# Column sums of the modulation rows: the rows as stationary operand against a column of ones, in place of a selector product, a copy and a transpose

## The chip, the core and the metric

The kernel runs on one core of one Trainium2 chip. The metric is the device time of one execution in microseconds (us), as a median of several runs. All arithmetic of the parts named here is in f32.

## What is computed

The program runs two layers of a diffusion backbone on 128 context tokens and 256 latent tokens. Before each sub-layer the normalised tokens are scaled and shifted by a modulation that depends on one vector per token group, `c_ctx` for the context and `c` for the latents. The part of the reference that matters here:

```
def modulate(h, shift, scale):
    return h * (1 + scale) + shift

def adaln(cvec, w, b):
    mod = jnp.einsum('nd,de->ne', jax.nn.silu(cvec), w) + b
    return jnp.split(mod[:, None, :], 6, axis=-1)

def trunk_layer(x, mods, mixer_w, g_norm_l, w_gu_l, w_down_l, ctx):
    sh1, sc1, ga1, sh2, sc2, ga2 = mods
    h = modulate(rms_norm(x, g_norm_l[0]), sh1, sc1)
    mix, new_ctx = token_mixers(h, *mixer_w, ctx)
    x = x + ga1 * rms_norm(mix, g_norm_l[1])
    f = swiglu(modulate(rms_norm(x, g_norm_l[2]), sh2, sc2), w_gu_l, w_down_l)
    x = x + ga2 * rms_norm(f, g_norm_l[3])
    return x, new_ctx
```

`w` is 1024 x 6144 in each layer. The six vectors sh1, sc1, ga1, sh2, sc2, ga2 are numbered 0 to 5 in the kernel (`vec`). Shifts and scales (0, 1, 3, 4) are wanted as columns, with the feature on the partition, since the tokens they act on lie transposed. The gates (2, 5) are wanted as rows.

## The kernel before

The class `Ada` computes the modulation piece by piece, in half vectors of 512 features. `issue` (L157 and on) loads four chunks of `w_ada`, 256 rows each. What follows depends on the stage.

In the token mixers `mul_p` multiplies on TensorE and sums over rows there; that path ends in `cols`, which the change splits in two without changing what it issues.

In the channel mixer (`ffn`) of both layers `mul_v` multiplies on ScalarE (the first row block) and VectorE (`scalar_tensor_tensor`, L179, seven for each of two token groups). The products pile up in `acc`, 128 partitions x 2 groups (`s`) x 512 features, which lies in one of two spare buffers (`spare` in the profile). Then the 128 partitions must be summed: `sum_v`. It takes eight f32 products, two groups `s` by four slices `g` of 128 features. The stationary operand is `pick`, 128 x 32, zero but for one column of ones; the moving operand is `acc`. Row `32 g + s` of the tile `adap` so receives the sum of slice g for group s. For a shift or scale VectorE then copies these rows to SBUF (L196), and one step later `cols` transposes them on TensorE (L233, tile `adat`) and adds the bias from the transposed tile into `Bmod` (L237) or `Amod` (L240, L242). For a gate VectorE adds a bias and `gate` goes on with the rows.

`ffn` of the first layer computes the gate 5 of its own layer and the vectors 0, 1, 3, 4 of the second layer, two halves each: ten calls of `sum_v`, two of them for gates. `ffn` of the second layer has the two gate halves alone. So the copy, the transpose and `cols` after a `sum_v` occur eight times in the program, all in the channel mixer of the first layer.

That stage also runs the channel mixer's own products. Each f32 value is split in a high and a low part (f32r), and each product takes three matmuls, `mm3` (L108 to L110): `gups` (gate and up, 128 x 384 tokens, weights from `ring` and `xring`) and `facc` (down, 128 x 512). ScalarE and VectorE split the weights into `hi` and `lo` or into the rings (L118, L119, L1209, L1210), and form `sg` and `f` between gate/up and down (L1223 to L1227).

What sets the order: `tick` issues one chunk, runs one deferred step from `later`, and then multiplies one chunk. In this stage a tick may do both. The stage is laid out by a scheduler; the instructions of each engine run in the order that it gives them, and each waits by semaphore for what it reads and for the buffer it writes. PSUM tiles `gups`, `adap` and `adat` share two buffers (tag `gu`), in turn.

Of the kernel before, what the change touches and what calls it, by code (L numbers as in the profile page):

```python
# [12 lines left out]
ALU = mybir.AluOpType  # L13
# [39 lines left out]
def hybrid_step(  # L53
# [8 lines left out]
    V, A, PE, G, SP = nc.vector, nc.scalar, nc.tensor, nc.gpsimd, nc.sync  # L62
# [17 lines left out]
    ident = cst[:, C_ID:C_ID + 128]  # L80
# [12 lines left out]
    gbn = cp.tile([128, 2, 2, 128], F32, name="gbn")  # L93
    G.memset(gbn, 0.0)
    pick = cp.tile([128, 33], F32, name="pick")
# [48 lines left out]
    class Ada:  # L144
# [38 lines left out]
            self.later += [lambda: self.sum_v(l, vec, half, acc)]  # L183

        def sum_v(self, l, vec, half, acc):
            ps = self.ps("adap")[:, 0:128]
            for s in range(2):
                for g in range(4):
                    PE.matmul(ps[32 * g:32 * g + 32], lhsT=pick[:, 1 - s:33 - s], rhs=acc[:, s, g * 128:(g + 1) * 128],
                              start=s == 0, stop=s == 1)  # L190
            rows = ap_.tile([128, 128], F32, tag="acc", name="acc", bufs=2)
            if vec in (2, 5):
                V.tensor_tensor(rows, ps, gbn[:, half, 0], ALU.add)
                self.gate(l, vec, half, rows)
            else:
                V.tensor_copy(rows, ps)  # L196
                self.later.insert(0, lambda: self.cols(l, vec, half, rows))

        def gate(self, l, vec, half, acc):

# [26 lines left out]
                    self.later += [lambda: self.cols(l, vec, half, acc)]  # L227

        def cols(self, l, vec, half, acc):
            which = 0 if vec < 3 else 1  # L230
            ks = slice(half * 4, half * 4 + 4)
            ps = self.ps("adat")
            PE.transpose(ps[:, 0:128], acc, ident)  # L233
            pv = ps[:, 0:128].rearrange("p (k r) -> p r k", k=4)[:, 0:2]
            bc = bcol[:, l, vec, ks].unsqueeze(1).broadcast_to([128, 2, 4])
            if vec in (0, 3):
                V.tensor_tensor(Bmod[:, l, which, :, ks], pv, bc, ALU.add)  # L237
            else:
                am = Amod[:, l, which, :, ks]
                V.tensor_tensor(am, pv, bc, ALU.add)  # L240
                gc = gcol[:, l, 2 * which, ks].unsqueeze(1).broadcast_to([128, 2, 4])
                V.scalar_tensor_tensor(am, am, 1.0, gc, ALU.add, ALU.mult)  # L242
# [1237 lines left out]
```

## Time and profile before

| what | us |
|---|---|
| median of 3 runs | 1000.54 |
| lowest and highest run | 1000.4, 1001.1 |
| the profiled execution's own time | 1001.41 |
| its span in the trace, first to last instruction | 999.6 |
| TensorE busy in the span | 966.1 |
| VectorE busy | 623.3 |
| ScalarE busy | 466.8 |

The profiled execution has 1.8 us outside its span. A busy TensorE is not TensorE at its peak: matmuls are pipelined, and the profile's rows overlap. What a piece costs on the path is therefore read from the chain of waits, whose rows do not overlap, and from the starts of consecutive matmuls, not from the length of a row. An f32 product appears as two weight loads (engine PEld) and two matmuls (engine PE); an f32r product and a transpose appear as one of each.

### The profile page before, as it was taken

To read this page: it belongs to the slowest core of one execution; us is meant where nothing else is said; L and a number is where in the kernel's file an instruction comes from. 1 tells how busy PE (TensorE), PEld (TensorE's weight loads), DVE (VectorE), ACT (ScalarE), POOL (GpSimd) and SP (SyncE) were. 2 spreads that over 40 slices of the span, in tenths; PEclk is the share of its full clock that TensorE was granted. 3 is DMA by queue.
4 is the path that set the end of the run, shared out by engine and by line. 5 is a ranking of instruction groups with operands and counts; after the bars stand their busy time and mean duration, and the time that the engine had idled before them with its cause. 6 is when DMAs were issued, how large, how long until landed. Compare 5 with 4: busy or idle time off the path is not lost.

```text
span 999.6 us, 16493 instructions
## 1 busy us (share of the span) xinstructions
PE 966.1 (97%) x6537; PEld 838.9 (84%) x6537; DVE 623.3 (62%) x1036; ACT 466.8 (47%) x930; POOL 85.8 (9%) x142
## 2 busy tenths in 40 slices
PE   5999999999999999999999999999999999999997
PEld 3789886668999999999987898766899999999996
DVE  3566657767964979986265757677787533333323
ACT  4545537678533433333266346577873323333322
POOL 0312320000000200000010343000000000000000
PEclk8999999999999999999999999999999999999999
DMA  9958678407873777763033794430575344333001
GB/s 327 314 175 255 207 211 237 150 1 253 277 231 126 265 256 236 252 229 110 22 100 107 189 283 122 110 106 1 191 270 192 127 149 148 127 127 127 22 1 64
DMA packets 128414, 167.30 MB, mean 167 GB/s; under 512 B 15600, under 2 KB 90080, under 8 KB 128336
## 3 DMA queue, kind: packets, MB, share of 16 engines
q1 hardware_dynamic: 122112, 154.00, 48.2%
q0 software_dynamic: 5856, 12.09, 4.4%
q8 instruction: 51, 0.84, 0.4%
q14 instruction: 27, 0.22, 0.1%
q10 hardware_dynamic: 368, 0.16, 0.1%
HBM read 163.51 MB, written 2.70 MB: 166 GB/s over the span
## 4 chain that ended last, share of the span: by engine, by line
PE 84%; ACT 5%; DVE 4%; DMA 3%; issue 2%; SPq 1%; POOL 0%; ACTq 0%; DVEq 0%; POOLq 0%
PE gups L108 11%; PE gups L110 11%; PE gups L109 11%; PE facc L108 6%; PE facc L110 6%; PE facc L109 6%; PE tps L108 3%; PE fps L108 2%; PE tps L110 2%; PE tps L109 2%; PE fps L110 2%; PE fps L109 2%; PE ops L108 2%; PE adap L214 2%; PE ptp L1031 2%
## 5 line engine op out<-in xcount | busy, mean ns | idle before, releaser
L119 DVE TENSOR_TENSOR lo<-raw,hi 128x1024 fp32r<-128x1024 f32 x98 | 119.1, 1221 | 65.9 <-ACT hi L118 62.4
L118 ACT ACTIVATE hi<-raw 128x1024 fp32r<-128x1024 f32 x98 | 103.2, 1058 | 93.5 <-PE facc L110 86.9
L108 PE MATMUL gups<-hT,ring 128*128 128x384 f32 x416 | 141.1, 339 | 0.0
L110 PE MATMUL gups<-hT,ring 128*128 128x384 f32 x416 | 140.6, 338 | 0.0
L109 PE MATMUL gups<-hT,ring 128*128 128x384 f32 x416 | 140.4, 338 | 0.0
L179 DVE SCALAR_TENSOR_TENSOR spare<-araw,scol,spare 128x512 f32<-128x512 f32 x168 | 115.6, 745 | 4.5 <-DMA araw<-in_w_ada_dram 4.5
L108 PE MATMUL facc<-hi,f 128*128 128x512 f32 x240 | 95.8, 399 | 0.0
L110 PE MATMUL facc<-hi,f 128*128 128x512 f32 x240 | 94.7, 394 | 0.0
L109 PE MATMUL facc<-lo,f 128*128 128x512 f32 x240 | 94.6, 394 | 0.0
L108 PEld LDWEIGHTS gups<-hT,ring 128*128 128x128 f32 x416 | 78.1, 188 | 0.9 <-issue 0.2
L109 PEld LDWEIGHTS gups<-hT,ring 128*128 128x128 f32 x416 | 78.1, 188 | 0.3
L110 PEld LDWEIGHTS gups<-hT,ring 128*128 128x128 f32 x416 | 78.1, 188 | 0.0
L108 PE MATMUL gups<-hT,xring 128*128 128x384 f32 x224 | 76.0, 339 | 0.0
L110 PE MATMUL gups<-hT,xring 128*128 128x384 f32 x224 | 75.7, 338 | 0.0
L109 PE MATMUL gups<-hT,xring 128*128 128x384 f32 x224 | 75.6, 338 | 0.0
L108 PE MATMUL tps<-hi,hT 128*128 128x512 f32 (+1 forms) x192 | 68.5, 357 | 2.6 <-DVE hT L486 2.6
L110 PE MATMUL tps<-hi,hT 128*128 128x512 f32 (+1 forms) x192 | 65.2, 339 | 0.0
L109 PE MATMUL tps<-lo,hT 128*128 128x512 f32 (+1 forms) x192 | 65.1, 339 | 0.0
L1209 ACT ACTIVATE ring<-spare 128x1024 fp32r<-128x1024 f32 x26 | 27.6, 1060 | 61.3 <-PE gups L109 35.5
L1209 ACT ACTIVATE ring<-rgu 128x1024 fp32r<-128x1024 f32 x26 | 27.6, 1061 | 60.3 <-PE gups L109 35.4
L1224 DVE TENSOR_TENSOR sg<-sg,gups 128x384 f32<-128x384 f32 x40 | 22.1, 552 | 53.7 <-PE gups L110 53.7
L108 PEld LDWEIGHTS facc<-hi,f 128*128 128x128 f32 x240 | 45.1, 188 | 11.2 <-issue 1.8
(304 smaller groups left out, 2018.2 us busy)
## 6 DMA issues: line engine op xcount, KB each, us to landing
araw<-in_w_ada_dram SPq DMA_DIRECT2D x80, 512.0 KB, 4.8
raw<-in_w_down_dram SPq DMA_DIRECT2D x44, 512.0 KB, 4.6
raw<-in_w_in_dram SPq DMA_DIRECT2D x40, 512.0 KB, 5.9
spare<-in_w_gu_dram SPq DMA_DIRECT2D x20, 1024.0 KB, 5.2
rgu<-in_w_gu_dram SPq DMA_DIRECT2D x20, 1024.0 KB, 5.7
sraw<-in_w_ada_dram SPq DMA_DIRECT2D x16, 512.0 KB, 9.8
raw<-in_w_out_dram SPq DMA_DIRECT2D x8, 512.0 KB, 6.3
G<-row POOLq DMA_DIRECT2D x8, 512.0 KB, 6.1
```

Source lines behind the costliest of these rows:

```text
L108: PE.matmul(out, lhsT=wh, rhs=xh, start=start, stop=False)
L109: PE.matmul(out, lhsT=wh, rhs=xl, start=False, stop=False)
L110: PE.matmul(out, lhsT=wl, rhs=xh, start=False, stop=stop)
L118: a = A.activation(hi[:, :n], raw, AF.Copy)
L119: v = V.tensor_tensor(lo[:, :n], raw, hi[:, :n].bitcast(F32), ALU.subtract)
L179: V.scalar_tensor_tensor(acc[:, s], raw[:, k2], scol[:, k, s:s + 1], acc[:, s], ALU.mult, ALU.add)
L214: PE.matmul(ps[32 * g:32 * g + 32], lhsT=scol[:, 2 * kk + k2], rhs=raw[:, k2, g * 128:(g + 1) * 128], start=k2 == 0, stop=k2 == 1)
L1031: PE.transpose(pt[:, hd, b * 128:(b + 1) * 128], self.P[:, hd, b * 128:(b + 1) * 128], ident)
L1209: A.activation(hi, rv, AF.Copy)
L1224: V.tensor_tensor(sg, sg, pu, ALU.mult)
```

## The change

For the vectors 0, 1, 3, 4, `sum_v` exchanges the operands. The stationary operand is a 128 x 128 slice of `acc`, and the moving operand is one column of ones, `pick[:, 1:2]`. Each of the eight products gives one column of `adat`: column `4 s + g` holds, on 128 partitions, the sums of slice g for group s. That is the form `cols` had after its transpose, so the bias is added at once by `add_cols`, the second half of the old `cols`. The copy to rows (L196), the deferred step and the transpose (L233 after a `sum_v`) go. The gate halves keep the old form, and so does the path of `mul_p`.

```
         def sum_v(self, l, vec, half, acc):
+            if vec not in (2, 5):
+                ps = self.ps("adat")
+                for s in range(2):
+                    for g in range(4):
+                        PE.matmul(ps[:, 4 * s + g:4 * s + g + 1], lhsT=acc[:, s, g * 128:(g + 1) * 128],
+                                  rhs=pick[:, 1:2], start=True, stop=True)
+                self.add_cols(l, vec, half, ps[:, 0:8].rearrange("p (r k) -> p r k", r=2))
+                return
             ps = self.ps("adap")[:, 0:128]
...
             rows = ap_.tile([128, 128], F32, tag="acc", name="acc", bufs=2)
-            if vec in (2, 5):
-                V.tensor_tensor(rows, ps, gbn[:, half, 0], ALU.add)
-                self.gate(l, vec, half, rows)
-            else:
-                V.tensor_copy(rows, ps)
-                self.later.insert(0, lambda: self.cols(l, vec, half, rows))
+            V.tensor_tensor(rows, ps, gbn[:, half, 0], ALU.add)
+            self.gate(l, vec, half, rows)
...
         def cols(self, l, vec, half, acc):
+            ps = self.ps("adat")
+            PE.transpose(ps[:, 0:128], acc, ident)
+            self.add_cols(l, vec, half, ps[:, 0:128].rearrange("p (k r) -> p r k", k=4)[:, 0:2])
+
+        def add_cols(self, l, vec, half, pv):
             which = 0 if vec < 3 else 1
             ks = slice(half * 4, half * 4 + 4)
-            ps = self.ps("adat")
-            PE.transpose(ps[:, 0:128], acc, ident)
-            pv = ps[:, 0:128].rearrange("p (k r) -> p r k", k=4)[:, 0:2]
             bc = bcol[:, l, vec, ks].unsqueeze(1).broadcast_to([128, 2, 4])
```

On TensorE, at the second of the eight sums (program order; `facc` is the down product, `f` its stationary operand), before:

```order
1550 L110 MATMUL facc_2884<-hi,f_3571 128x512
1551 L189 MATMUL adap<-spare_2706,pick 32x128 x8
1552 L108 MATMUL facc_2879<-hi,f_3631 128x512
1553 L109 MATMUL facc_2879<-lo,f_3631 128x512
1554 L110 MATMUL facc_2879<-hi,f_3632 128x512
1555 L233 MATMUL adat<-cst,acc 128x128
1556 L108 MATMUL facc_2880<-hi,f_3631 128x512
```

and now:

```order
1549 L110 MATMUL facc_2884<-hi,f_3571 128x512
1550 L190 MATMUL adat<-pick,spare_2706 128x1 x8
1551 L108 MATMUL facc_2879<-hi,f_3631 128x512
1552 L109 MATMUL facc_2879<-lo,f_3631 128x512
1553 L110 MATMUL facc_2879<-hi,f_3632 128x512
1554 L108 MATMUL facc_2880<-hi,f_3631 128x512
```

The eight products stand where they stood, between the same matmuls, and the transpose is gone.

On VectorE, from the second sum past the third (L1210 and L1216 split weights into a ring, L119 splits down weights, L1224 and L1230 form `sg`), before:

```order
373 L196 COPY acc<-adap 128x128
374 L119 TENSOR_TENSOR lo<-raw,hi 128x1024
375 L237 TENSOR_TENSOR Bmod<-adat,bcol 128x2x4
376 L179 SCALAR_TENSOR_TENSOR spare_2706<-araw,scol,spare_2706 128x512 x5
377 L196 COPY acc<-adap 128x128
378 L179 SCALAR_TENSOR_TENSOR spare_2706<-araw,scol,spare_2706 128x512
379 L240 TENSOR_TENSOR Amod<-adat,bcol 128x2x4
380 L179 SCALAR_TENSOR_TENSOR spare_2706<-araw,scol,spare_2706 128x512
381 L242 SCALAR_TENSOR_TENSOR Amod<-Amod,gcol 128x2x4
382 L179 SCALAR_TENSOR_TENSOR spare_2706<-araw,scol,spare_2706 128x512 x7
383 L1210 TENSOR_TENSOR ring<-rgu,ring 128x1024
```

and now:

```order
372 L243 TENSOR_TENSOR Bmod<-adat,bcol 128x2x4
373 L119 TENSOR_TENSOR lo<-raw,hi 128x1024
374 L179 SCALAR_TENSOR_TENSOR spare_2706<-araw,scol,spare_2706 128x512 x4
375 L246 TENSOR_TENSOR Amod<-adat,bcol 128x2x4
376 L179 SCALAR_TENSOR_TENSOR spare_2706<-araw,scol,spare_2706 128x512
377 L248 SCALAR_TENSOR_TENSOR Amod<-Amod,gcol 128x2x4
378 L179 SCALAR_TENSOR_TENSOR spare_2706<-araw,scol,spare_2706 128x512 x6
379 L1216 TENSOR_TENSOR ring<-rgu,ring 128x1024
```

The two copies are gone. `Bmod` and `Amod` now read the sum itself, at the places of the copies or one multiplication earlier, and three multiplications moved behind the ring's split.

## Rows read from the trace of the kernel before

**Rows 1.** The page: busy time by engine; the chain's shares by engine.

```profile
PE 966.1 (97%) x6537; PEld 838.9 (84%) x6537; DVE 623.3 (62%) x1036; ACT 466.8 (47%) x930; POOL 85.8 (9%) x142
...
PE 84%; ACT 5%; DVE 4%; DMA 3%; issue 2%; SPq 1%; POOL 0%; ACTq 0%; DVEq 0%; POOLq 0%
```

**Rows 2.** Stretches: length; busy PE, PEld, DVE, ACT, POOL; granted clock; DMA.

```profile
16.50:23.20 6.70, 5.55 (x58) 4.33 (x62) 2.48 (x5) 1.17 (x3) 0.00 (x0) 0.50 1.09 356
...
320.00:485.00 165.00, 165.00 (x983) 149.38 (x982) 132.66 (x196) 58.05 (x76) 8.34 (x14) 1.00 0.63 211
...
637.00:641.00 4.00, 2.57 (x42) 1.83 (x38) 3.71 (x6) 3.17 (x10) 0.00 (x0) 1.00 0.11 27
```

**Rows 3.** Chain, 373.6 to 376.2 us (second sum): start, us, what.

```profile
374.20 0.57 PE adap L189 x16
374.78 0.43 PE facc L108
375.20 0.23 PE facc L109
...
375.66 0.11 PE adat L233
```

**Rows 4.** VectorE in order of time, 370 to 402 us (second and third sum).

```profile
374.84 0.29 DVE L196 COPY acc<-adap 128x128 f32<-128x128 f32 x1 [2.12 <-PE adap L189]
375.33 1.23 DVE L119 TENSOR_TENSOR lo<-raw,hi 128x1024 fp32r<-128x1024 f32 x1 [0.20 <-ACT hi L118]
...
376.55 3.39 DVE L179 SCALAR_TENSOR_TENSOR spare<-araw,scol,spare 128x512 f32<-128x512 f32 x5
...
386.88 1.23 DVE L1210 TENSOR_TENSOR ring<-rgu,ring 128x1024 fp32r<-128x1024 f32 x1 [0.24 <-ACT ring L1209]
```

**Rows 5.** Chain, 126.0 to 129.2 us: products with 65 and 130 moving columns.

```profile
126.54 0.39 PE nd L907 x4
126.93 0.28 PE nd L903 x2
127.21 0.84 PE nd L907 x8
128.05 0.28 PE nd L903 x2
128.33 0.39 PE nd L907 x4
128.72 0.23 PE fps L108
128.95 0.18 PE fps L109
```

**Rows 6.** Chain, 31.4 to 33.6 us: products with 4 moving columns, then transposes.

```profile
32.02 0.34 PE scp L297 x4
32.36 0.71 PE trp L476 x6
```

**Rows 7.** Groups by line and shape: count, busy us, mean ns, idle before.

```profile
L297 PE MATMUL scp<-cst,srows 128*128 128x4 f32 x16 | 2.3, 239 | 0.1
...
L297 PEld LDWEIGHTS scp<-cst,srows 128*128 128x128 f32 x16 | 2.4, 189 | 0.6 <-ACT srows L296 0.4
```

**Rows 8.** Matmuls in order of time, at four places: start, us, idle before.

```profile
17.65 0.80 PE L108 MATMUL tps<-hi,hT 128*128 128x512 f32 x1 [2.56 <-DVE hT L486]
...
31.63 0.39 PE L110 MATMUL tps<-hi,hT 128*128 128x512 f32 x1
...
389.36 0.34 PE L108 MATMUL gups<-hT,ring 128*128 128x384 f32 x1
...
640.22 1.10 PE L1002 MATMUL sc<-share 64*64 64x128 f32 x32 [1.43 <-ACT P L1016]
```

**Rows 9.** Weight loads in order of time, 31.6 to 33.2 us: start, us.

```profile
31.63 0.64 PEld L297 LDWEIGHTS scp<-cst,srows 128*128 128x128 f32 x4
32.11 0.72 PEld L476 LDWEIGHTS trp<-cst,xn 128*128 128x128 f32 x6
```

## The prediction

> **What bounds the kernel now.** I read the page first: TensorE is busy 966.1 of 999.6 us, and of the chain of work that ended last 84% is TensorE's [rows 1]. A share of the whole says nothing of one stage, so I then asked for the stretch in which the changed sums lie, 320 to 485 us, the channel mixer of the first layer. There TensorE is busy in all of its 165.00 us, at the full granted clock of 1.00, while VectorE has 132.66 us of work and ScalarE 58.05 [rows 2]. The reader is to see that nothing keeps TensorE waiting there: what is added to its queue in this stretch makes the run longer, and what is taken from the others makes it no shorter. Since a busy matmul row overlaps the next, I took prices from the chain, whose pieces follow one another without overlap, first around a sum that goes, then around blocks of products that look like the ones that come.
>
> **What goes.** Around the second of the eight sums the chain gives 0.57 us to the sixteen matmuls of L189, and the `facc` behind them takes 0.43 where its neighbour takes 0.23, because its weights can't be loaded early; the transpose takes 0.11 [rows 3]. So one sum with its transpose now costs 0.57 + 0.20 + 0.11 = 0.88 us of TensorE, and eight cost 7.0. The old form is cheap because four products of 32 stationary columns lie side by side in the array. The eight copies on VectorE go as well, 8 x 0.29 = 2.3 us [rows 4]. I count them as nothing: TensorE never waits for VectorE in this stretch [rows 2]. If that cover were gone, they would be worth 2.3 us at most.
>
> **What comes.** Eight f32 products with 128 x 128 stationary values and one moving column; as f32 goes in two passes, 16 weight loads and 16 matmuls in a row. No row of before has one moving column. The nearest by count of columns is L297, with 4; the longest clean block is L907 and L903, with 65 and 130.
>
> The long block: 20 loads and matmuls take 0.39 + 0.28 + 0.84 + 0.28 + 0.39 = 2.18 us on the chain, and the `fps` behind them 0.23 where its neighbour takes 0.18 [rows 5], together 2.23 us or 0.1115 us for each. The narrow products alone are a little under that (0.84 / 8 = 0.105) and the wide ones a little over. Half the columns save so little because the weight loads set the pace, and with one column they are still the same loads. 16 x 0.1115 = 1.78 us for a sum.
>
> The short block: four products of 4 columns take 0.34 and the six transposes behind them 0.71 us [rows 6], 1.05 for ten or 0.105 for each. 16 x 0.105 = 1.68 us. That is the low end; some of it belongs to transposes, whose loads are shorter. The high end is the 1.78 plus one weight load that is not hidden behind the `facc` before it, 0.19 us [rows 7], which is 1.97. I take 1.78, because the block is of the same kind from end to end and returns to the same kind of product; that the first load is hidden I take from the short block, where it starts at 31.63 with the matmul ahead of it [rows 8, 9].
>
> The sum: 1.78 - 0.88 = +0.90 us for each, from +0.80 to +1.09. Eight of them make +7.2 us, from +6.4 to +8.7. All of it is on TensorE, which sets the end, so nothing is taken off for cover. Against the profiled execution's own time that is 1001.41 + 7.2 = 1008.6. That execution is 0.87 us above the median of the runs; the difference is the same for both, so the median should be 1000.54 + 7.2 = 1007.7, from 1006.9 to 1009.2.
>
> The Trainium skill has a rule for the price of a load, "TensorE: Matmul & The Clock Gate", section "LDWEIGHTS (loading the stationary operand)": the time follows the count of stationary columns, at 1.2 columns a nanosecond, and not the rows. It speaks against this change, which goes from 32 to 128 such columns. By it, as an estimate, a load is 107 ns, a sum 1.71, and the time 1007.1; the block's 0.1115 us agrees but for its last 5 ns.
>
> Other edits. `add_cols` does the same one or two small additions as `cols` did, from another tile: nothing. The deferred step after the sum goes, so a tick comes free; the order shows no DMA queue changed but for one `rgu` load that passes one `araw` load, twice, and the `gups` weights are then asked for earlier, not later: nothing. One PSUM buffer of the two is taken instead of two. The `gups` behind the sum therefore waits for the one reader of `adat`, and before it waited for the copy and the addition: nothing, as long as VectorE gets there in the 4 us that the first `gups` tile runs.
>
> **Rivals.**
>
> *VectorE is held by the longer sum, and then holds TensorE.* `Bmod` and `Amod` read the sum itself now, and VectorE runs in order: behind a waiting `Amod` stand the multiplications and the split of the next ring weights, for which `gups` waits. At the second sum: it would end at 374.20 + 1.78 = 376.0 [rows 3], `Bmod` after it; the split of L119 takes 1.23 and four multiplications 4 x 0.68 = 2.7 [rows 4], so VectorE reaches `Amod` at about 380.1. TensorE runs 18 `facc` of 0.23 first and ends the third sum at about 376.0 + 4.2 + 1.8 = 382.0. VectorE stands still for some 2 us, then does seven multiplications (4.8) and the ring's split (1.23), and is done at about 388.2. The `gups` that needs it starts at 389.36 now [rows 8] and would at about 391.2. That leaves 3 us. If they were used up, by a late `araw` chunk say, the 2 us would show on TensorE at both places where two sums lie close: 1007.7 + 4.2 = 1011.9. Chance 6%.
>
> *The clock falls in the sums.* From 16.5 to 23.2 us the granted clock is 0.50 [rows 2], that is 1.2 GHz, and a wait of 2.56 us lies ahead of the matmul at 17.65 [rows 8]. In a sum 1.78 us would pass with only 16 columns moving. Against it: with TensorE wholly idle for 1.43 us ahead of 640.22 [rows 8] the clock stays at 1.00 [rows 2], that is 2.4 GHz, and here the array keeps loading. If it fell each time for as long as in that row, half of 6.70 us would be lost eight times: 1007.7 + 26.8 = 1034.5. Chance 3%.
>
> *Loads don't overlap matmuls.* Each pair would then take a load and a matmul in series, 0.19 + 0.24 us [rows 7], a sum 16 x 0.43 = 6.9, and the run 1000.54 + 8 x (6.9 - 0.88) = 1048.7. Against it: the first load of L297 begins at 31.63 [rows 9], with the matmul of L110 that begins at 31.63 [rows 8] and fills all rows of the array, and the long block's 0.11 us is less than one load. The Trainium skill says otherwise, same page, part 3 on packing small matmuls, "The mechanism": a load overlaps a matmul in flight only when they use different row groups. No pair here does, and the rows don't bear it out. Chance 1%.
>
> *Not slower: with one column to move, loads follow faster.* The place is inside each sum, and the point is 0.88 / 16 = 0.055 us a load: below it the change gains. One pair of loads in the trace is that close: the last of L297 starts at 31.63 + 0.64 - 0.19 = 32.08, and the first of L476 at 32.11 [rows 9], 0.03 later. At that pace a sum would take 0.48 and the run 1000.54 - 3.2 = 997.3. Against it: the loads of L476 that follow are again (0.72 - 0.14) / 5 = 0.12 apart on that row, so the head start is not kept, and four moving columns already leave the matmuls nothing to hold the loads back with. Chance 2%, half of it near no change.
>
> **How the numbers follow.** The forecast, 1007.7, has 88%. Its own bounds are 1006.9 to 1009.2. The range reaches 0.7 us below, about the spread of the runs shown, and above to 1010.4, part of the way to VectorE's rival; the clock and the serial loads stay outside. A measurement of this kernel can tell a change from none at about 0.2%, 2 us. Forecast and three rivals lie above that: slower 0.98; no change 0.01, faster 0.01.
>
> **What the profile after would show.** The row of the new products (L190) with 128 loads and 128 matmuls, and no copy from `adap` at all. On the chain a block of 16 of them with 1.7 to 1.8 us, its `facc` neighbours at 0.23. The starts of the two `facc` around a sum tell it best. The stretch of the channel mixer 7 us longer, with TensorE busy throughout and the clock at 1.00, and all other stages as long as before. Wrong in size if the pairs come at another pace than 0.11 us; wrong in kind if a wait for VectorE stands ahead of a `gups`, if the clock shows 0.50 inside the stage, or if another stage gives time back.

## The result, and the profile after

The changed kernel takes 1008.12 us (median of 6 runs, 1007.47 to 1010.77), the kernel before in the same comparison 1000.60. The ratio is 1.0074, with a 95% interval from 1.0057 to 1.0090: slower by 5.7 to 9.0 us. The forecast was 1007.7, with 1006.2 to 1010.4 as its range. The profiled execution of after takes 1007.82 us, with a span of 1006.0. One thing is needed to read the times below: five of the profiles hold a stretch of 6.83 us at half the clock near 107 us, ahead of all that was changed, which costs up to 3.4 us, and the text names them; the executions of the kernel before fall into two groups, about 1001 and 1004 us, which would fit it, but no profile of before holds it.

First the page of after: busy time, share of the span and count of instructions by engine, and then the shares of the chain that ended last.

```profile
PE 972.9 (97%) x6529; PEld 850.1 (84%) x6529; DVE 621.4 (62%) x1028; ACT 466.9 (46%) x930; POOL 83.8 (8%) x142
PE 84%; ACT 5%; DVE 4%; DMA 3%; issue 2%; SPq 1%; POOL 0%; ACTq 0%; DVEq 0%; POOLq 0%
```

Against [rows 1] TensorE is busy 6.8 us longer, with 8 instructions fewer, while VectorE has 1.9 us less to do and 8 instructions fewer. The time did not follow VectorE.

The stretch of the channel mixer in the first layer, 7 us longer than in [rows 2] (its length, then busy time and count for PE, PEld, DVE, ACT and POOL, the granted clock, the DMA share and GB/s):

```profile
320.00:492.00 172.00, 172.00 (x974) 160.69 (x973) 131.23 (x188) 58.32 (x76) 8.31 (x14) 1.00 0.62 202
```

TensorE is busy in all of it, as before, and the granted clock is 1.00. The list of what TensorE waited for in that stretch is empty. Next the chain around the second sum (start, us, what), the counterpart of [rows 3]:

```profile
374.80 0.23 PE facc L110
375.03 1.68 PE adat L190 x16
376.71 0.34 PE facc L108
377.05 0.23 PE facc L109
```

Sixteen products of one column take 1.68 us. The `facc` behind them takes 0.34 where its neighbours take 0.23, so the sum costs 1.68 + 0.11 = 1.79 us of TensorE, or 0.112 us for each weight load; by the starts of the matmuls all eight sums of the stage cost the same within 0.01 us. The groups of the new line (busy us, mean ns of one, idle time before):

```profile
L190 PEld LDWEIGHTS adat<-pick,spare 128*128 128x128 f32 x128 | 15.5, 191 | 0.7
L190 PE MATMUL adat<-pick,spare 128*128 128x1 f32 x128 | 14.7, 245 | 0.0
```

A load lasts 191 ns by its row and a matmul 245, and yet there is one pair every 112 ns: each overlaps its neighbours. The chain shows the pace and the rows don't. Last, VectorE after the second and third sums, to be read beside [rows 4] (the bracket is the idle time ahead, and what ended it):

```profile
376.75 0.17 DVE L243 TENSOR_TENSOR Bmod<-adat,bcol 128x8 f32<-128x8 f32 x1 [3.18 <-PE adat L190]
...
382.71 0.17 DVE L246 TENSOR_TENSOR Amod<-adat,bcol 128x8 f32<-128x8 f32 x1 [2.01 <-PE adat L190]
...
388.02 1.23 DVE L1216 TENSOR_TENSOR ring<-rgu,ring 128x1024 fp32r<-128x1024 f32 x1 [0.44 <-ACT ring L1215]
```

Before, the same `Amod` waited 0.26 us:

```profile
381.10 0.17 DVE L240 TENSOR_TENSOR Amod<-adat,bcol 128x8 f32<-128x8 f32 x1 [0.26 <-PE adat L233]
```

VectorE now stands still for 2.01 us there. Nothing comes of it: the split of the ring ends at 389.25, and the `gups` that reads it starts at 391.07:

```profile
391.07 0.34 PE L108 MATMUL gups<-hT,ring 128*128 128x384 f32 x1
```

One thing came otherwise. Behind the stage a product that started at 597.93 starts at 605.02, 7.1 us later, but the product of [rows 8] that started at 640.22 is only 6.4 us later:

```profile
605.02 1.00 PE L913 MATMUL nd<-share,W 128*128 128x65 f32 x8
...
646.61 1.10 PE L1008 MATMUL sc<-share 64*64 64x128 f32 x32 [1.43 <-ACT P L1022]
```

So the token mixers of the second layer, which the change leaves alone, give 0.7 us back. TensorE waits there for VectorE's `W`, twice, 1.6 us in all before and 1.0 now. On the way to the second of these waits VectorE needs less time for two multiplications, first of before and then of after:

```profile
611.06 1.02 DVE L659 TENSOR_TENSOR t<-z,ropes 128x64 f32<-128x64 f32 x2
```

```profile
618.14 0.35 DVE L665 TENSOR_TENSOR t<-z,ropes 128x64 f32<-128x64 f32 x2
```

In the f32r run below, which takes as long as before, the same two also take 0.35 us, so it is not the longer sums that shorten them. The profiled execution of before is 0.87 us above the median of its runs, which would fit a trait of that one execution; whether it is that, or goes with the order that the change left, one profile of before can't tell.

### The profile page after: what moved, and what is told of

The parts are those of the page before. It is cut to its first block, busy times and chain, and to the rows that moved or that the text cites. A ratio compares the mean times of both kernels' runs of the same rounds, so it can differ in the third digit from the quotient of the medians.

```text
span 1006.0 us, 16469 instructions
## 1 busy us (share of the span) xinstructions
PE 972.9 (97%) x6529; PEld 850.1 (84%) x6529; DVE 621.4 (62%) x1028; ACT 466.9 (46%) x930; POOL 83.8 (8%) x142
## 4 chain that ended last, share of the span: by engine, by line
PE 84%; ACT 5%; DVE 4%; DMA 3%; issue 2%; SPq 1%; POOL 0%; ACTq 0%; DVEq 0%; POOLq 0%
PE gups L108 11%; PE gups L110 11%; PE gups L109 11%; PE facc L108 6%; PE facc L110 6%; PE facc L109 6%; PE tps L108 3%; PE fps L108 2%; PE tps L110 2%; PE tps L109 2%; PE fps L110 2%; PE fps L109 2%; PE ops L108 2%; PE adap L218 2%; PE ptp L1037 2%
## 5 line engine op out<-in xcount | busy, mean ns | idle before, releaser
L119 DVE TENSOR_TENSOR lo<-raw,hi 128x1024 fp32r<-128x1024 f32 x98 | 119.2, 1221 | 68.5 <-ACT hi L118 65.1
L1230 DVE TENSOR_TENSOR sg<-sg,gups 128x384 f32<-128x384 f32 x40 | 22.1, 553 | 52.5 <-PE gups L110 52.3
```

Of the source, the lines that this page charges most:

```text
L119: v = V.tensor_tensor(lo[:, :n], raw, hi[:, :n].bitcast(F32), ALU.subtract)
L1230: V.tensor_tensor(sg, sg, pu, ALU.mult)
```

## The experiments

Theory: the change costs the pace of its weight loads, 16 x 0.112 us in each sum against 0.88, on an engine that has no cover. Its rivals: a price paid once for each sum, the moving columns, VectorE's longer waits, and the clock. The edits are shown against the changed kernel.

**Twice the products.**

```diff
+                for n in range(2):
                     for s in range(2):
                         for g in range(4):
-                            PE.matmul(ps[:, 4 * s + g:4 * s + g + 1], lhsT=acc[:, s, g * 128:(g + 1) * 128],
+                            o = 8 * (1 - n) + 4 * s + g
+                            PE.matmul(ps[:, o:o + 1], lhsT=acc[:, s, g * 128:(g + 1) * 128],
...
```

> The changed kernel with the eight products of each of the eight sums issued twice, the first time into eight columns of the bank that nobody reads. It adds 16 weight loads and 16 matmuls of one column to each sum and changes nothing else. Theory (the change costs what its weight loads take on TensorE, 0.112 us for each of 128 columns, with no cover): +1.79 us for a sum, +14.3 us in all, 1008.1 + 14.3 = 1022.4 us; the block of a sum on TensorE goes from 1.79 to 3.58. Rival 1 (most of the price is paid once for a sum, on entering and leaving the narrow products): clearly under +10 us, below 1018. Rival 2 (VectorE, held at the sums, has a part in the price): VectorE's wait at Amod grows from 2.0 to about 3.8 us and a gups waits for the ring: more than 1024, with a wait of TensorE in the stretch from 320 to 500 us.

Measured: 1036.75 us, ratio 1.0344 (1.0317 to 1.0371), 14 us above the theory. The chain around the first sum, and VectorE at the same two places as above:

```profile
351.35 3.46 PE adat L192 x32
354.82 0.34 PE facc L108
```

```profile
383.68 0.17 DVE L245 TENSOR_TENSOR Bmod<-adat,bcol 128x8 f32<-128x8 f32 x1 [4.97 <-PE adat L192]
...
392.98 0.17 DVE L248 TENSOR_TENSOR Amod<-adat,bcol 128x8 f32<-128x8 f32 x1 [5.35 <-PE adat L192]
```

The block is what the theory said: 3.46 + 0.11 = 3.57 us, twice 1.79, with nothing paid once. VectorE is held for 5 us at either place, and the list of TensorE's waits is empty here too, so rival 2 is out. What is over shows in the granted clock, behind the second and third sums and at the fourth:

```profile
379.80:383.53 3.73, 3.73 (x35) 3.69 (x33) 0.00 (x0) 1.78 (x2) 0.00 (x0) 1.00 0.77 264
383.53:386.94 3.41, 3.41 (x9) 2.74 (x10) 3.27 (x6) 0.73 (x1) 0.00 (x0) 0.50 0.28 72
386.94:393.77 6.83, 6.83 (x49) 6.34 (x49) 1.48 (x5) 1.06 (x1) 0.00 (x0) 1.00 0.33 120
393.77:397.18 3.41, 3.41 (x12) 3.41 (x12) 3.41 (x8) 0.00 (x0) 0.00 (x0) 0.50 0.36 101
```

```profile
417.66:424.49 6.83, 6.83 (x24) 5.96 (x24) 4.13 (x8) 1.44 (x2) 0.00 (x0) 0.50 0.22 69
```

TensorE is busy without a gap, and still the clock goes to 1.2 GHz. There are six such stretches, five of 3.41 us and one of 6.83. Five begin within 1.4 us behind the block of a sum (the second, third, fifth, seventh and eighth); the long one begins inside the fourth block, which takes 4.67 us on the chain in place of 3.46:

```profile
415.65 4.67 PE adat L192 x32
```

At half the clock they lose up to 23.9 / 2 = 11.9 us; this profile also holds the stretch near 107 us, up to 3.4. With 8 x (3.57 - 0.88) = 21.5 for the loads that makes at most 36.8, and the profiled execution, 1036.27, is 34.9 above that of before. So the prediction's rival of the clock is real, though not at the size that the change has.

**32 moving columns in place of one.**

```diff
-                        PE.matmul(ps[:, 4 * s + g:4 * s + g + 1], lhsT=acc[:, s, g * 128:(g + 1) * 128],
-                                  rhs=pick[:, 1:2], start=True, stop=True)
+                        o = 32 * (4 * s + g)
+                        PE.matmul(ps[:, o:o + 32], lhsT=acc[:, s, g * 128:(g + 1) * 128],
+                                  rhs=pick[:, 1:33], start=True, stop=True)
...
```

> The changed kernel with 32 moving columns in each new product in place of one; the one column that is wanted is read out of every 32. Weight loads as before, 31 times more columns to move. Theory (the loads set the pace, the matmuls run beside them): the pairs stay 0.112 us apart, 1008.1 us, within 1. Rival (the moving columns count, added to a fixed time): the long block of the kernel before, where 130 columns in place of 65 stretched a pair from 0.105 to about 0.12 us, gives 0.015 / 65 = 0.0002 us a column, 31 columns x 128 pairs x 0.0002 = +0.9 us; if the matmul were on the path wholly, at one column a cycle of 2.4 GHz, 31 x 128 / 2400 = +1.7 us, 1009.8, and at four times that +6.6, 1014.7.

Measured: 1009.64 us (1007.99 to 1010.98), ratio 1.0074, the same as that of the change. The profile holds the stretch near 107 us; the chain:

```profile
378.18 1.71 PE adat L191 x16
379.89 0.31 PE facc L108
```

1.71 + 0.08 = 1.79 us again. Thirty-one columns more cost nothing in the block. The median alone lies nearer to a rival's 1009.8 than to 1008.1, but two of the four executions, 1007.99 and 1008.59, are within 0.5 us of the theory.

**Half as many loads: the single-pass type f32r.** The last multiplication writes an f32r tile, and the column of ones goes with one of zeros as two moving columns.

```diff
-                        PE.matmul(ps[:, 4 * s + g:4 * s + g + 1], lhsT=acc[:, s, g * 128:(g + 1) * 128],
-                                  rhs=pick[:, 1:2], start=True, stop=True)
+                        o = 2 * (4 * s + g)
+                        PE.matmul(ps[:, o:o + 2], lhsT=acc[:, s, g * 128:(g + 1) * 128],
+                                  rhs=pickr[:, 0:2], start=True, stop=True)
...
```

> The changed kernel with the eight sums in the single-pass type f32r: the last multiplication of each writes an f32r tile, and the products have 128 x 128 of it stationary and two moving columns (zeros and ones). Eight weight loads and eight matmuls in a sum in place of sixteen, of the same shape; the sums are less precise. Theory (the price is the count of loads times 0.112 us): a sum of 8 x 0.112 = 0.89 us, 8 x 0.89 = 7.1 us less, 1001.0 us, no different from the kernel before. Rival 1 (a load goes by its bytes or its type, so one f32r load takes as long as the two passes of f32): 1008.1. Rival 2 (a fixed time for a sum is part of the 1.79): between the two, for instance 1002.2 if 0.3 us of a sum are fixed.

Measured: 1001.11 us, ratio 0.9991 (0.9976 to 1.0007): no different from before. The chain:

```profile
374.88 0.79 PE adat L196 x8
375.66 0.34 PE facc L110
```

0.79 + 0.11 = 0.90 us for eight loads, each with its matmul: half the pairs, half the price.

**The same eight products in bfloat16.** As the last, with bfloat16 for f32r and one moving column.

> As the run in f32r, but the last multiplication writes bfloat16 and the moving column of ones is bfloat16: eight loads and eight matmuls in a sum, at half the bytes; the multiplied rows are rounded to bfloat16 before the sum. Theory (the count of loads of 128 columns sets the price, whatever the type): as in f32r, 0.89 us for a sum, 1001.0 us. Rival (a load goes by its bytes): half of that again, 0.45 us for a sum, 1008.1 - 8 x 1.34 = 997.4 us, which would be faster than before.

Measured: 999.5 us (996.87 to 1002.66), ratio 0.9977 (0.9960 to 0.9994), a little faster than before. TensorE around the second sum, and its weight loads there:

```profile
375.56 0.40 PE L112 MATMUL facc<-hi,f 128*128 128x512 f32 x1
375.80 0.35 PE L195 MATMUL adat<-pickr,accr 128*128 128x1 bf16 x8
376.01 0.48 PE L110 MATMUL facc<-hi,f 128*128 128x512 f32 x1
376.33 0.39 PE L111 MATMUL facc<-lo,f 128*128 128x512 f32 x1
```

```profile
375.79 0.27 PEld L195 LDWEIGHTS <-accr 128*128 128x128 bf16 x8 [0.27 <-issue]
```

From 375.56 to 376.33 are 0.77 us, of which two `facc` are 0.46: the sum costs 0.31. The row of one load is 95 ns, so the eight start (0.27 - 0.095) / 7 = 0.025 us apart, not 0.111 and not half of it. Both sides of the expectation were too slow. The Trainium skill has a possible reason, "TensorE: Matmul & The Clock Gate", section "Weight-path perf modes — Fast Weight Load (FWL) and DoubleRow": weights of 128 columns in a type other than FP32 are loaded in four chunks at once. A quarter of its 107 ns would be 27, an estimate from that page, and the run's 25 fits it, though the same table has a gain of about two as measured, and not of four. That this is the cause is not shown: the matmuls of the block follow every 0.025 us as well, and which of the two sets the pace no run separates. The f32r run keeps the pace of f32. Of the 8 x (0.88 - 0.31) = 4.6 us, 1.5 arrived in the medians. The profiled execution, 1000.44, holds the stretch near 107 us, and TensorE now waits for VectorE and ScalarE in the stretch (who waited for whom, us, times, longest):

```profile
PE gups L110 <- DVE sg L1235: 1.1, 2, 0.7
PE gups L110 <- ACT sg L1234: 0.3, 1, 0.3
```

These waits come to 1.4 us; where the rest was lost is open.

**Only the shifts.** The sums of vec 1 and 4 go back to the old form.

```diff
-            if vec not in (2, 5):
+            if vec in (0, 3):
```

> Only the four sums of the shifts (vec 0 and 3) take the new form, the four of the scales (1 and 4) keep the old one. Theory (each sum costs by itself, on TensorE, 1.79 - 0.88 = +0.91 us): four of them +3.6 us over the kernel before, 1000.7 + 3.6 = 1004.3 us; new blocks of 1.79 us, old ones of 0.57 with 0.11 for the transpose. Rival (VectorE's wait at Amod, the place where two sums lie close, has a part in the 7.5 us): with the scales in the old form that wait is another one, so the price is not half: under +2 or over +5.

Measured: 1004.49 us against 1001.47, ratio 1.0026 (1.0013 to 1.0040), that is +1.3 to +4.0 us around the 3.6. This interval reaches below the rival's +2, so the chain has to decide. At the second sum it has the new pieces, and at the third the old ones again, 0.57, 0.43 and 0.11, as [rows 3]:

```profile
374.81 1.68 PE adat L190 x16
376.48 0.34 PE facc L108
...
380.77 0.57 PE adap L197 x16
381.35 0.43 PE facc L108
...
382.24 0.11 PE adat L239
```

Each sum pays by itself, and TensorE waits for nothing in the stretch.

**64 stationary columns.**

```diff
-                        PE.matmul(ps[:, 4 * s + g:4 * s + g + 1], lhsT=acc[:, s, g * 128:(g + 1) * 128],
-                                  rhs=pick[:, 1:2], start=True, stop=True)
+                        for h in range(2):
+                            PE.matmul(ps[64 * h:64 * h + 64, 4 * s + g:4 * s + g + 1],
+                                      lhsT=acc[:, s, g * 128 + 64 * h:g * 128 + 64 * h + 64],
+                                      rhs=pick[:, 1:2], start=True, stop=True)
```

> The changed kernel with each new product split in two of 64 stationary columns, which go to partitions 0 to 63 and 64 to 127 of the bank: 32 weight loads of 64 columns in a sum in place of 16 of 128, the same columns in all. Theory A (a load costs by its stationary columns): 0.056 us a pair, a sum 1.8 us as before, 1008.1 us, perhaps 0.3 us more in a sum for entering and leaving the other tile size, 1010.5 at most. Theory B (each load has a fixed time of 0.11 us): 32 x 0.112 = 3.57 us for a sum, +14.3, 1022.4; and if the granted clock falls behind such long blocks as it did with 32 loads of 128 columns, up to 1036.7.

Measured: 1004.0 us (1002.75 to 1011.87), ratio 1.0027 (1.0009 to 1.0046): less than either theory. The profile holds the stretch near 107 us. The chain, and the weight loads of the block:

```profile
377.28 1.03 PE adat L191 x32
378.31 0.43 PE facc L108
```

```profile
377.20 1.01 PEld L191 LDWEIGHTS adat<-pick,spare 128*64 128x64 f32 x32 [0.37 <-issue]
```

1.03 + 0.20 = 1.23 us for as many columns as took 1.79. In the trace the loads start two at a time, 7 ns apart. The row of one is 138 ns, so the sixteen twos are (1.01 - 0.138) / 15 = 0.058 us apart, 0.93 in all. That is theory A's price for a load of 64 columns, but the two halves are loaded side by side, which I had not reckoned with. The other 0.3 us goes into entering and leaving the smaller tile (the loads idle for 0.37 us ahead of the block, and the `facc` behind takes 0.43).

**32 stationary columns,** with four products in place of two:

```diff
+                        for h in range(4):
+                            PE.matmul(ps[32 * h:32 * h + 32, 4 * s + g:4 * s + g + 1],
+                                      lhsT=acc[:, s, g * 128 + 32 * h:g * 128 + 32 * h + 32],
+                                      rhs=pick[:, 1:2], start=True, stop=True)
```

> The changed kernel with each new product split in four of 32 stationary columns, at partitions 0, 32, 64 and 96 of the bank: 64 weight loads of 32 columns in a sum, still with one moving column. In the run with 64 columns the loads of the two column halves went side by side, a pair of them every 0.058 us, and a sum took 1.23 us with about 0.3 for entering and leaving the smaller tile. Theory (a load costs by its columns, and column groups load side by side): 16 steps of 0.029 and 0.3, 0.76 us for a sum, 8 x (0.76 - 0.88) = -1.0 us against the kernel before, 1000.2 us. Rival (TensorE's queue passes an instruction in no less than the 0.0065 us seen between neighbours there, eight to a step): 16 x 0.052 + 0.3 = 1.13, +2.0 us, 1003.2.

Measured: 1001.21 us against 1001.16, ratio 0.9998 (0.9986 to 1.0010). The chain, where a few records are missing (58 of 64), and the matmuls of the block:

```profile
374.72 0.64 PE adat L191 x58
375.36 0.43 PE facc L108
```

```profile
374.65 0.71 PE L191 MATMUL adat<-pick,spare 128*32 128x1 f32 x64
```

0.64 + 0.20 = 0.84 us: the theory's 0.76 and 0.08 more, and far from the rival's 1.13. So the form that the change wants, in f32 and without the copy and the transpose, costs what the old one did, once its weights go through four column groups. It does not beat it by anything that can be measured.

**Twice the products, with 32 moving columns.** The two edits together.

> The doubled kernel (32 pairs in each sum) with 32 moving columns in each product in place of one. In the doubled kernel the blocks took 3.57 us each, as forecast, but the granted clock stood at 0.50 for some 3.4 to 6.8 us behind six of the eight, and the whole was 36 us over before in place of 21. Theory A (the clock falls because hardly a column moves in these 3.6 us): with 32 times as many columns and the same pace of loads the clock stays at 1.00 and the time is 1008.1 + 14.3 = 1022.4 us. Theory B (the clock falls whenever narrow products stand that long, whether 1 or 32 columns move): 1036.7 us again, with the same stretches at 0.50.

Measured: 1032.18 us, ratio 1.0284 (1.0261 to 1.0308). The clock falls here too, at four sums in place of six (the second, fourth, sixth and eighth; at the last it falls inside the block). The first two of the four:

```profile
383.68:387.09 3.41, 3.41 (x10) 2.67 (x9) 3.41 (x5) 0.54 (x1) 0.00 (x0) 0.50 0.38 92
...
417.80:421.22 3.42, 3.42 (x10) 2.65 (x9) 3.42 (x7) 0.37 (x1) 0.00 (x0) 0.50 1.02 312
```

Theory A is out. Theory B's time was not reached either, as there are four stretches of 3.41 us and none of 6.83: 21.5 for the loads, up to 6.8 for these and up to 3.4 for the stretch near 107 us, which this profile holds, make at most 31.7, and its 1032.04 is 30.6 above before. Why four and not six is open.

**Half as many products again:** 24 loads in a sum.

```diff
-                for s in range(2):
+                for s in (0, 0, 1):
```

> The changed kernel with the four products of the first batch row issued twice in each sum: 24 weight loads and matmuls in place of 16 (the kernel with 32 lost the clock behind six of eight sums, that with 16 behind none). If the clock stays at 1.00: 24 x 0.1115 = 2.68 us for a sum, 8 x 0.89 = +7.1 over the changed kernel, 1015.2 us. If it falls as with 32: some 12 us more, 1027.

Measured in two executions, 1016.57 and 1026.88 us, with a mean granted clock of 0.995 and 0.984: it seems that both cases occurred, though the faster one left no profile. In the profiled one, the slower, the clock stood at 0.50 in seven stretches of the channel mixer, at every sum but the fourth. Two begin inside a block; where none does, the pace of the loads is unchanged (2.57 + 0.11 = 2.68). One of the seven, and the chain ahead of it:

```profile
377.28 2.57 PE adat L190 x24
379.85 0.34 PE facc L108
```

```profile
381.15:384.57 3.42, 3.42 (x9) 2.63 (x8) 2.69 (x5) 0.00 (x0) 0.00 (x0) 0.50 0.64 177
```

**The copies put back.** A copy of 128 x 128 that nobody reads stands on VectorE in each sum.

```diff
+                back = ap_.tile([128, 128], F32, tag="acc", name="acc", bufs=2)
+                V.tensor_copy(back, acc[:, 0, 0:128])
```

> The changed kernel with the copy of 128 x 128 on VectorE put back into each of the eight sums, as work that nobody reads (0.29 us each, 2.3 us in all). Theory (VectorE's work in this stretch is hidden, its copies were worth nothing): 1008.1 us, within 1. Rival (the copies that went gave time back, so that the products really cost more than +7.5): +2.3 us, 1010.4.

Measured: 1010.04 us (1008.14 to 1011.50), ratio 1.0071 (1.0048 to 1.0093), beside 1.0074 for the change. The median alone would fit the rival, but in this comparison the kernel before is 0.9 us longer as well, and the profiled execution, 1008.14 with a span of 1006.4, is within 0.4 us of that of after. The copies read SBUF and took less than those removed:

```profile
L193 DVE COPY acc<-spare 128x128 f32<-128x128 f32 x8 | 1.8, 221 | 0.0
```

A gain from 1.8 us of copies would have been near the limit of what this comparison tells. That nothing on TensorE waits is the better evidence.

## Why the prediction was right

- **What bounds the kernel.** TensorE is busy in all of the stretch before and after, and the experiments that changed its blocks moved the time by about their sum, as long as the clock stood. Bfloat16 is the exception: of 4.6 us only 1.5 arrived, and there TensorE waits.
- **What goes: 0.88 us.** The old pieces stand unchanged in the run with the shifts alone. The reason given, that four products of 32 columns lie side by side, is borne out by the run with 32 columns: the new products, split in the same way, fall from 1.79 to 0.84 us.
- **What comes: 16 x 0.1115 = 1.78 us.** It is 1.79. The pace was taken from a block with 65 and 130 moving columns, and the step from there to one column held because the loads set the pace. The run with 32 moving columns rules out these columns. A load and its matmul come as a pair in every run, but the runs with 64 and 32 stationary columns rule out a fixed price of a pair, since there a pair takes 0.93 / 32 = 0.029 us and at most 0.64 / 64 = 0.010. What is left is the stationary columns and, as bfloat16 shows, their type. The first load starts 0.23 us ahead of its block, with the `facc` before it, so it is hidden as was taken. The Trainium skill's 107 ns for a load of 128 columns ("TensorE: Matmul & The Clock Gate", "LDWEIGHTS (loading the stationary operand)") is 5 ns short of this pace, and its rule by columns is as close at 64 (53 ns by the rule, an estimate, against the 58 of the run).
- **The sum: +7.2 us.** Eight blocks of 1.79 make 8 x 0.91 = +7.3, the stage is 7.1 us longer by the trace, and the medians differ by 7.5. The profiled executions differ by 6.4 alone, since the second layer gives 0.7 us back. "If another stage gives time back" was a sign of being wrong in kind; it came, but by the rows it goes back mostly to one slow place in the profile of before, whose cause is open, and not to the sums. The prediction's step from the profiled execution to the median was too simple, too: that of before lies 0.87 us above its median, that of after 0.30 below. How close 1007.7 came to 1008.12 is in part luck; the price of a sum is not.
- **VectorE's rival.** The 2 us at `Amod` came as reckoned. The margin behind it was put at 3 us and is 391.07 - 389.25 = 1.8: `gups` comes as reckoned, but the split ends a microsecond later, since the working started the second sum at 374.20 and left out the 0.83 us by which the first had moved it (375.03). With the wait at 5.35 us, in the doubled kernel, TensorE still waits for nothing, but its own work is later there by as much; a wait of VectorE alone was not tried.
- **Loads in series, and loads that are faster.** Rows of 191 and 245 ns at a pace of 112 rule out the first for f32. Faster loads do occur, but with the type (0.025 us in bfloat16) or the column groups, and not with the single column from which I had it.
- **The clock's rival.** No stretch at 0.50 lies in the channel mixer of after. But the 3% were argued from the wrong side: I looked for an idle TensorE, as ahead of 17.65 in [rows 8], and in the runs with 24 and 32 loads it falls behind or inside blocks in which TensorE is busy throughout. With half as many products again it fell in the one execution that was profiled, and in the other, by its time, it seems to have stood.

## What to carry to other kernels

Price a block of narrow f32 products by its weight loads, not by its moving columns, and take the pace from starts along the chain, since rows of loads and matmuls overlap. If the big operand must be the stationary one, split it over four groups of 32 columns, or take bfloat16 if the sums allow it; here it then cost no more than the form that it replaces. And where a kernel that is bound by TensorE gets more such blocks, read the granted clock behind them as well as their own length.

## What the runs showed of the hardware that I had not expected

- The granted clock went from 1.00 to 0.50 behind or inside unbroken blocks of 24 and 32 narrow f32 weight loads (2.7 and 3.6 us), for 3.41 or 6.83 us at a time, and in no profile at those of 16 (1.79 us). With 32 loads it did so at four of eight blocks with 32 moving columns and at six of eight with one, and the two executions with 24 loads differ by 10.3 us. What decides in the single case is open.
- A 128 x 128 weight load in bfloat16 follows its neighbour after 0.025 us, in f32r after 0.112, as long as one of the two f32 passes.
- Loads of 64 columns went two at a time every 0.058 us.
- A stretch at half the clock comes and goes ahead of all that was changed. The profiles with 64 stationary columns, in bfloat16, with 32 moving columns and of both doubled kernels hold it. The first row is of the run with 32 moving columns, the second of the changed kernel.

```profile
106.60:113.50 6.90, 6.73 (x31) 6.76 (x32) 3.90 (x12) 2.96 (x7) 1.54 (x3) 0.51 0.82 267
```

```profile
106.60:113.50 6.90, 6.74 (x89) 6.15 (x90) 5.37 (x14) 3.44 (x9) 2.36 (x4) 1.00 1.03 309
```
